# Storing the filter features by residue instead of in order of position

## The chip, the cores and the metric

The kernel runs on one core of a Trainium2 chip. The metric is the device time of one execution in microseconds; lower is better.

## The reference

One layer of a hybrid block on x (1 x 2048 x 1024): RMS norm, an input projection to 3072 columns, a short convolution, a second-order Hyena operator (two long convolutions by FFT with generated filters, each multiplied by a gate), a multi-scale pooling branch, and an output projection with a residual. The change touches the generation of the filters only:

```python
    h = jnp.sin(freq * (z @ w1 + b1))
    h = jnp.sin(freq * (h @ w2 + b2))
    h = jnp.sin(freq * (h @ w3 + b3))
    h = (h @ w_proj).reshape(L, HYENA_ORDER, N_DIRECTIONS, HYENA_WIDTH)
    ...
    return h * decay[:, None, None, :]
```

`h` before its last product are the features: 64 numbers for each of L = 2048 positions. Each position's features times `w_proj` (64 x 2048) and times a decay give the filters of two orders, two directions and 512 channels, which then go through the FFT.

## The kernel before

The work goes in this order: the projection with its pooling and gate parts (to about 400 us), the rest of the projection in natural layout with the short convolution (lines 493 to 571, to about 600 us), and then the long convolutions, in four units of an order and a half of the channels (lines 795 to 837), with the output projection of the pooling branch (`fill`, lines 783 to 793) spread between. A planner places the instructions in each engine's queue by priorities, data and its own estimates, so lines of different parts are interleaved; each engine runs its queue in order.

The features are computed early (`mlp`, line 433) and kept in DRAM as `h_d`. While the third block of the natural projection runs (`ch == 2`, lines 495 to 507), they are read back in four pieces of 512 positions, on both halves of the partitions: partitions 0 to 63 of the table `HT` get the features rounded to fp32r (ScalarE, line 506), partitions 64 to 127 the remainder of that rounding (VectorE, line 507). `HT` holds the positions in order, with 16 columns of zero behind them (line 497). The staging tile `hb` has one buffer, whose place a split weight half (line 230) uses before and after.

The FFT wants position 16 a + r by residue r. So `pre_k` (line 606) generates for residue n2 with a stationary operand of 128 columns at a step of 16, one for each direction, and the two halves of the split weights:

```python
                    c0 = n2 if dr == 0 else 16 - n2
                    lh = HT[:, c0:c0 + 2033:16]
                    for k_, wt in enumerate((wh, wl)):
                        T.matmul(ps[:, dr], lh, wt[:, dr * 256:dr * 256 + 256], start=(k_ == 0), stop=(k_ == 1))
```

These four matmuls (the group of one residue) fill one PSUM bank `gen` of 128x512. VectorE multiplies it by the decay into `ab` (line 631); two residues make a pass `m`, of which GpSimd forms the sum (line 635) and VectorE the difference (line 636) of the directions; two products with the transform matrix `f1` follow (`s1k`, line 643), one evacuated by ScalarE and one by VectorE (line 644). `gen` and `s1k` share two PSUM banks (tag "k"). After eight passes VectorE transposes the result in 32x32 blocks (line 604) and the unit's loop over frequencies (`gloop`, lines 669 to 718: `pk`, `px`, `pc`) begins. In the first unit the passes stand nearly alone; in the others they are interleaved with `gloop`, with the next stage's transforms (`s`, `py`) and with `fill` (`fp`).

The natural projection itself (`nm`, lines 540 to 542) is 24 matmuls of 128x256 for each of 16 row blocks, in a ring of six PSUM banks, evacuated by three products on VectorE (line 547). The convolution's neighbours over the block's edge come by two shifted row loads (`a0p`, line 550, `a2p`, line 556), issued by the queue of SyncE as soon as VectorE has made their source.

Of the kernel before, what the change touches and what calls it, by code (L numbers as in the profile page):

```python
# [10 lines left out]
F32 = mybir.dt.float32  # L11
F32R = mybir.dt.float32r
I32 = mybir.dt.int32
AF = mybir.ActivationFunctionType
ALU = mybir.AluOpType

P = 128
L = 2048
# [3 lines left out]
R = 16  # L22
# [126 lines left out]
def build(tc, I, out, debug=None):  # L149
    nc = tc.nc  # L150
    V, S, G, T, Q = nc.vector, nc.scalar, nc.gpsimd, nc.tensor, nc.sync
# [334 lines left out]


    hp = pool(hst, "hp", 1, None, "right")
    HT = hp.tile([P, L + 16], F32R, name="HT")
    nat = ExitStack()  # L490
    sn = pool(nat, "sn", 1, None, "right")
    psN = pool(nat, "psN", 1, PS, "right")
    for ch in range(4):
        load_w(ci)
        if ch == 2:

            V.memset(HT[:, L:L + 16].bitcast(F32), 0.0)
            for b in range(2):
                for q in range(2):
                    hb = sn.tile([P, 2, 512], F32R, tag="wh4", name=f"hb{b}{q}", bufs=1)  # L500
                    hs, hh = hb[:, 0].bitcast(F32), hb[:, 1]
                    for hf in range(2):
                        S.dma_start(out=hs[64 * hf:64 * hf + 64], in_=h_d[64 * b:64 * b + 64, q * 512:q * 512 + 512])
                    sl = slice(b * 1024 + q * 512, b * 1024 + q * 512 + 512)
                    S.copy(out=hh, in_=hs)
                    S.copy(out=HT[0:64, sl], in_=hh[0:64])
                    V.tensor_tensor(out=HT[64:128, sl], in0=hs[64:128], in1=hh[64:128], op=ALU.subtract)
        wc = sn.tile([P, 4, 256], F32, tag="wc", name=f"wc{ch}", bufs=1)
        for s in range(3):
            Q.dma_start(out=wc[:, s], in_=I["cw"][s:s + 1, ch * 256:ch * 256 + 256].broadcast_to([P, 256]))  # L510
        Q.dma_start(out=wc[:, 3], in_=I["cb"][:, ch * 256:ch * 256 + 256].broadcast_to([P, 256]))
        dst = g0_d[ch % 2]

        def store(r, t):

            if ch > 1:
                Q.dma_start(out=dst[:, r:r + 4], in_=t)
                return
            hi = sn.tile([P, 4, 256], F32R, tag="vh", name=f"vh{ch}_{r}", bufs=1)
            S.copy(out=hi, in_=t)  # L520
            G.tensor_tensor(out=t, in0=t, in1=hi, op=ALU.subtract)
            for k, a in enumerate((hi.bitcast(F32), t)):
                for i in range(2):
                    for c in range(2):
                        Q.dma_start(out=v_d[ch, r // 2 + i, c, :, k],
                                    in_=a[:, 2 * i:2 * i + 2, 128 * c:128 * c + 128])

        a0p = sn.tile([P, 256], F32, tag="a0p", name=f"a0p{ch}", bufs=1)
        a2p = sn.tile([P, 256], F32, tag="a2p", name=f"a2p{ch}", bufs=1)
        t15 = sn.tile([P, 256], F32, tag="t15", name=f"t15{ch}", bufs=1)  # L530
        G.memset(a0p, 0.0)
        G.memset(a2p, 0.0)
        prev0 = prevt = ot = pot = None
        for l2 in [15] + list(range(15)):
            ps = psN.tile([P, 256], F32, tag="nm", name=f"nm{ch}_{l2}", bufs=6)
            xh, xl = XH[l2 // 4], XL[l2 // 4]
            ls = slice((l2 % 4) * 128, (l2 % 4) * 128 + 128)
            for d in range(NT):
                wh, wl = wcache[ci][0][d]
                T.matmul(ps, xh[:, d, ls], wh, start=(d == 0), stop=False)  # L540
                T.matmul(ps, xh[:, d, ls], wl, start=False, stop=False)  # L541
                T.matmul(ps, xl[:, d, ls], wh, start=False, stop=(d == NT - 1))  # L542
            if l2 == 0:
                load_w(ci + 1, sn)
            a = [sn.tile([P, 256], F32, tag=f"a{s}", name=f"a{s}_{ch}_{l2}", bufs=(3, 1, 3)[s]) for s in range(3)]
            for s in range(3):
                V.scalar_tensor_tensor(out=a[s], in0=ps, scalar=r_nat[:, l2:l2 + 1], in1=wc[:, s],  # L547
                                       op0=ALU.mult, op1=ALU.mult)
            if l2 == 15:
                Q.dma_start(out=a0p[1:128], in_=a[0][0:127])  # L550
                G.tensor_tensor(out=t15, in0=a[1], in1=wc[:, 3], op=ALU.add)
                a2_15 = sn.tile([P, 256], F32, tag="a215", name=f"a215{ch}", bufs=1)
                S.copy(out=a2_15, in_=a[2])
                continue
            if l2 == 0:
                Q.dma_start(out=a2p[0:127], in_=a[2][1:128])
            if l2 % 4 == 0:
                ot = sn.tile([P, 4, 256], F32, tag="ot", name=f"ot{ch}_{l2}", bufs=2)
            tt = sn.tile([P, 256], F32, tag="tt", name=f"tt{ch}_{l2}", bufs=3)
            V.tensor_tensor(out=tt, in0=a[1], in1=wc[:, 3], op=ALU.add)  # L560
            G.tensor_tensor(out=tt, in0=tt, in1=(a0p if l2 == 0 else prev0), op=ALU.add)
            if l2 > 0:
                G.tensor_tensor(out=pot[:, (l2 - 1) % 4], in0=prevt, in1=a[2], op=ALU.add)
                if l2 % 4 == 0:
                    store(l2 - 4, pot)
            prev0, prevt, pot = a[0], tt, ot
        G.tensor_tensor(out=pot[:, 2], in0=prevt, in1=a2_15, op=ALU.add)
        G.tensor_tensor(out=t15, in0=t15, in1=prev0, op=ALU.add)
        G.tensor_tensor(out=pot[:, 3], in0=t15, in1=a2p, op=ALU.add)
        store(12, pot)  # L570
        ci += 1
# [29 lines left out]
    def trans(B, cbs=range(8)):  # L601
        for cb in cbs:
            ap = B[:, :, cb * 32:cb * 32 + 32].rearrange("p a c i -> p c a i")
            V.transpose(out=ap, in_=ap)  # L604

    def pre_k(o, hf):
        u = f"{o}{hf}"
        kw = wp.tile([P, 1024], F32, tag="wraw", name=f"kw{u}", bufs=1)
        wr, hd = kw[:, 0:512], kw[0:1, 512:768]
        for h in range(2):  # L610
            Q.dma_start(out=wr[64 * h:64 * h + 64].rearrange("p (a c) -> p a c", a=2), in_=I["fwo"][:, o, :, hf])
        Q.dma_start(out=hd, in_=I["hd"][o:o + 1, hf * 256:hf * 256 + 256])
        wh = hp.tile([P, 512], F32R, tag="kwh", name=f"kwh{u}", bufs=1)
        wl = hp.tile([P, 512], F32R, tag="kwl", name=f"kwl{u}", bufs=1)
        S.copy(out=wh, in_=wr)
        V.tensor_tensor(out=wl, in0=wr, in1=wh, op=ALU.subtract)
        sds = {}

        def gen(m):
            dc = kp.tile([P, 2, 2, 256], F32, tag="dec", name=f"dec{u}_{m}", bufs=2)  # L620
            (S if u == "00" and m < 2 else Q).dma_start(out=dc, in_=I["t_dec"][hf, m])
            ab = abp.tile([P, 2, 2, 256], F32, tag="ab", name=f"ab{u}_{m}", bufs=2)
            for i in range(2):
                n2 = 2 * m + i
                ps = psB.tile([P, 2, 256], F32, tag="k", name=f"gen{u}_{n2}", bufs=2)
                for dr in range(2):
                    c0 = n2 if dr == 0 else 16 - n2
                    lh = HT[:, c0:c0 + 2033:16]
                    for k_, wt in enumerate((wh, wl)):
                        T.matmul(ps[:, dr], lh, wt[:, dr * 256:dr * 256 + 256], start=(k_ == 0), stop=(k_ == 1))  # L630
                V.tensor_tensor(out=ab[:, i], in0=ps, in1=dc[:, i], op=ALU.mult)  # L631
                if n2 == 0:
                    G.tensor_tensor(out=ab[0:1, 0, 0], in0=ab[0:1, 0, 0], in1=hd, op=ALU.add)
            sd = wp.tile([P, 2, 2, 256], F32, tag="wh", name=f"sd{u}_{m}", bufs=3)
            G.tensor_tensor(out=sd[:, 0], in0=ab[:, :, 0], in1=ab[:, :, 1], op=ALU.add)  # L635
            V.tensor_tensor(out=sd[:, 1], in0=ab[:, :, 0], in1=ab[:, :, 1], op=ALU.subtract)
            sds[m] = sd

        def s1k(m):
            sd = sds.pop(m)  # L640
            for ri in range(2):
                ps = psB.tile([P, 2, 256], F32, tag="k", name=f"s1k{u}_{m}_{ri}", bufs=2)
                T.matmul(ps, f1[:, ri], sd[:, ri], start=True, stop=True)  # L643
                (V.tensor_copy if ri else S.copy)(out=BK[:, ri * 8 + m].rearrange("p c i -> p i c"), in_=ps)

        for m in range(9):
            if m < 8:
                gen(m)
            if m:
                s1k(m - 1)  # L650
        trans(BK)
# [171 lines left out]
    op = pool(ost, "op", 1, None, "right")  # L823
# [122 lines left out]
```

## Time and profile before

| | us |
|---|---|
| median of 3 runs | 1264.46 (1262.76 to 1265.32) |
| the profiled execution | 1265.64, of which its span 1263.9 |
| TensorE busy | 1179.0 (93%) |
| VectorE busy | 860.1 (68%) |
| ScalarE busy | 440.3 (35%) |
| GpSimd busy | 469.6 (37%) |
| mean granted TensorE clock | 0.980 |

The busy time of TensorE counts matmuls that overlap, so 93% does not mean that the array is at its peak. Weight loads are listed as an engine of their own (PEld) and run beside the matmul before them. What a stage is worth is read from the chain of work that ended last and from the timeline of that stage. In the rows, L630 is line 630; `gen<-kwl,HT` is an instruction that writes the tile `gen` from `kwl` and `HT`; "x4" merges four of a kind; what stands in brackets is how long the engine was idle before it and who ended that.

### The profile page before, as it was taken

The page shows a single profiled execution, that of the slowest core. Times are in us where ns is not written, and L with a number is a line of the kernel's source. Part 1 is how long each engine was busy: PE and PEld are TensorE (multiplying, and loading weights), DVE is VectorE, ACT ScalarE, POOL GpSimd, SP SyncE. Part 2 cuts the span into 40 slices and gives each one's busy share as a digit, 9 for nine tenths or more (in the row PEclk, how much of TensorE's full clock was granted, in tenths as well). Part 3 has the DMA queues.
Part 4 walks back from the last instruction along what each step waited for, and adds up shares of the span by engine and source line. Part 5 has one row for each costly group of instructions (what it writes and reads, how often), then busy time and mean ns, then how long its engine had stood idle before and what let it go on. Part 6 is the DMA issues. An engine that isn't in the chain of part 4 may idle for free.

```text
span 1263.9 us, 16966 instructions
## 1 busy us (share of the span) xinstructions
PE 1179.0 (93%) x6040; PEld 974.8 (77%) x6040; DVE 860.1 (68%) x1419; ACT 440.3 (35%) x724; POOL 469.6 (37%) x416
## 2 busy tenths in 40 slices
PE   8799999999999999899979999999999999988894
PEld 6688888787887999899666786778777767677683
DVE  6865347446346567576678887784868874769887
ACT  7612111112112111100148463742375624833321
POOL 3202021404452477566515332421234321434544
PEclk9899999999999999999999999999999999999997
DMA  7214131321341353423675346537664457554764
GB/s 256 86 37 132 34 100 40 118 87 59 128 153 51 117 140 91 142 95 140 238 234 156 97 136 192 136 95 251 194 176 107 123 185 233 116 181 145 244 215 147
DMA packets 110628, 177.25 MB, mean 140 GB/s; under 512 B 11076, under 2 KB 58960, under 8 KB 109264
## 3 DMA queue, kind: packets, MB, share of 16 engines
q1 hardware_dynamic: 108720, 173.20, 44.6%
q10 hardware_dynamic: 1648, 2.44, 0.6%
q8 instruction: 48, 0.79, 0.3%
q0 software_dynamic: 176, 0.53, 0.1%
q14 instruction: 36, 0.29, 0.1%
HBM read 113.75 MB, written 44.56 MB: 125 GB/s over the span
## 4 chain that ended last, share of the span: by engine, by line
PE 58%; DVE 16%; DMA 10%; issue 7%; ACT 4%; POOL 4%; SPq 1%; DVEq 0%; ACTq 0%; POOLq 0%
PE mm L317 8%; PE mm L319 8%; PE mm L318 8%; PE gen L630 4%; PE pc L704 3%; PE s1k L643 3%; DMA a2p<-a 3%; PE pk L678 3%; PE px L690 2%; PE fp L768 2%; PE nm L540 2%; PE nm L542 2%; PE nm L541 2%; PE fp L769 2%; PE fp L770 2%
## 5 line engine op out<-in xcount | busy, mean ns | idle before, releaser
L540 PE MATMUL nm<-wh,XH 128*128 128x256 f32 x512 | 145.9, 285 | 6.0 <-DVE a L547 5.2
L542 PE MATMUL nm<-wh,XL 128*128 128x256 f32 x512 | 145.5, 284 | 0.0
L541 PE MATMUL nm<-wl,XH 128*128 128x256 f32 x512 | 145.2, 284 | 0.0
L696 POOL TENSOR_TENSOR xs<-xs,kk 128x512 f32<-128x512 f32 x64 | 84.8, 1328 | 118.9 <-ACT xs L693 81.5
L547 DVE SCALAR_TENSOR_TENSOR a<-nm,r_nat,wc 128x256 f32<-128x256 f32 x192 | 81.5, 475 | 50.0 <-DMA wc<-cw 14.6
L540 PEld LDWEIGHTS nm<-wh,XH 128*128 128x128 f32 x512 | 97.9, 191 | 6.9 <-DVE a L547 6.0
L317 PE MATMUL mm<-XH,wh 128*128 128x512 f32 x256 | 103.0, 403 | 0.0
L319 PE MATMUL mm<-XH,wl 128*128 128x512 f32 x256 | 102.2, 399 | 0.0
L635 POOL TENSOR_TENSOR sd<-ab 128x512 f32<-128x512 f32 x32 | 53.0, 1656 | 131.4 <-DVE ab L631 131.0
L318 PE MATMUL mm<-XL,wh 128*128 128x512 f32 x256 | 101.5, 396 | 0.0
L541 PEld LDWEIGHTS nm<-wl,XH 128*128 128x128 f32 x512 | 97.9, 191 | 0.0
L542 PEld LDWEIGHTS nm<-wh,XL 128*128 128x128 f32 x512 | 97.7, 191 | 0.0
L704 PE MATMUL pc<-yt,gi 128*128 128x256 f32 x256 | 69.7, 395 | 13.3 <-DVE BS L705 8.3
L604 DVE STREAM_TRANSPOSE BS<-BS 128x1024 f32<-128x1024 f32 x64 | 73.5, 1210 | 8.5 <-ACT BS L659 8.5
L695 DVE TENSOR_TENSOR yt<-px,kk 128x512 f32<-128x512 f32 x64 | 44.0, 688 | 43.1 <-ACT xs L693 24.6
L690 PE MATMUL px<-BS,gf 128*128 128x256 f32 x256 | 70.2, 395 | 3.1 <-DVE yt L695 1.6
L678 PE MATMUL pk<-BK,gf 128*128 128x256 f32 x256 | 70.9, 389 | 0.0
L704 PEld LDWEIGHTS pc<-yt,gi 128*128 128x128 f32 x256 | 45.0, 191 | 32.7 <-DVE BS L705 15.7
L659 ACT COPY BS<-s 128x512 f32<-128x512 f32 x64 | 39.9, 629 | 83.1 <-PE s L588 79.4
L643 PE MATMUL s1k<-sd,f 128*128 128x512 f32 x128 | 63.2, 603 | 2.6 <-POOL sd L635 2.6
L697 DVE TENSOR_TENSOR yt<-yt,xs 128x512 f32<-128x512 f32 x64 | 53.9, 843 | 12.9 <-POOL xs L696 10.7
L317 PE MATMUL mm<-XH,whz 128*128 128x512 f32 x128 | 54.2, 424 | 9.0 <-ACT XH L284 5.3
(208 smaller groups left out, 3153.3 us busy)
## 6 DMA issues: line engine op xcount, KB each, us to landing
kk<-kk SPq DMA_DIRECT2D x128, 128.0 KB
fy<-yp_d SPq DMA_DIRECT2D x32, 512.0 KB
dec<-t_dec SPq DMA_DIRECT2D x30, 512.0 KB
wr<-w SPq DMA_DIRECT2D x16, 512.0 KB
ut<-v_d SPq DMA_DIRECT2D x32, 256.0 KB
gt<-g_d SPq DMA_DIRECT2D x32, 256.0 KB
op_d<-fo SPq DMA_DIRECT2D x32, 256.0 KB
o<-op_d SPq DMA_DIRECT2D x32, 256.0 KB
```

Of the source, the lines that this page charges most:

```text
L317: T.matmul(ps, wh, XH[lb][:, d], start=(d == 0), stop=False)
L318: T.matmul(ps, wh, XL[lb][:, d], start=False, stop=False)
L319: T.matmul(ps, wl, XH[lb][:, d], start=False, stop=(d == NT - 1))
L540: T.matmul(ps, xh[:, d, ls], wh, start=(d == 0), stop=False)
L541: T.matmul(ps, xh[:, d, ls], wl, start=False, stop=False)
L542: T.matmul(ps, xl[:, d, ls], wh, start=False, stop=(d == NT - 1))
L547: V.scalar_tensor_tensor(out=a[s], in0=ps, scalar=r_nat[:, l2:l2 + 1], in1=wc[:, s], op0=ALU.mult, op1=ALU.mult)
L643: T.matmul(ps, f1[:, ri], sd[:, ri], start=True, stop=True)
L678: T.matmul(pk[:, i], gf[:, gs[m] + i], BK[:, gs[m] // 2, :, i], start=True, stop=True)
L690: T.matmul(px[:, i], gf[:, gs[m] + i], BS[:, gs[m] // 2, :, i], start=True, stop=True)
L696: G.tensor_tensor(out=xs, in0=xs, in1=kk[:, 1], op=ALU.mult)
L704: ins = T.matmul(pc[:, i], gi[:, gs[m] + i], yt[:, i], start=True, stop=True)
```

## The change

The table `HT` becomes 16 rows of 129 columns: column a of row r is position 16 a + r. The 129th column of row 0 is set to zero; of the other rows it is neither written nor read. The copies that fill the table read their piece with a step of 16 positions and write 32 neighbouring columns of each of the 16 rows. The stationary operand of `gen` is then 128 neighbouring columns of one row, beginning at column 0, or at column 1 of row 0 for position 16. The values, the number of instructions and the size of the table (2064 columns) stay as they are.

```diff
--- before.py
+++ after.py
@@ -486,7 +486,7 @@
 
 
     hp = pool(hst, "hp", 1, None, "right")
-    HT = hp.tile([P, L + 16], F32R, name="HT")
+    HT = hp.tile([P, R, 129], F32R, name="HT")
     nat = ExitStack()
     sn = pool(nat, "sn", 1, None, "right")
     psN = pool(nat, "psN", 1, PS, "right")
@@ -494,17 +494,18 @@
         load_w(ci)
         if ch == 2:
 
-            V.memset(HT[:, L:L + 16].bitcast(F32), 0.0)
+            V.memset(HT[:, 0, 128:129].bitcast(F32), 0.0)
             for b in range(2):
                 for q in range(2):
                     hb = sn.tile([P, 2, 512], F32R, tag="wh4", name=f"hb{b}{q}", bufs=1)
                     hs, hh = hb[:, 0].bitcast(F32), hb[:, 1]
                     for hf in range(2):
                         S.dma_start(out=hs[64 * hf:64 * hf + 64], in_=h_d[64 * b:64 * b + 64, q * 512:q * 512 + 512])
-                    sl = slice(b * 1024 + q * 512, b * 1024 + q * 512 + 512)
+                    sl = slice(b * 64 + q * 32, b * 64 + q * 32 + 32)
                     S.copy(out=hh, in_=hs)
-                    S.copy(out=HT[0:64, sl], in_=hh[0:64])
-                    V.tensor_tensor(out=HT[64:128, sl], in0=hs[64:128], in1=hh[64:128], op=ALU.subtract)
+                    hs, hh = (a.rearrange("p (l r) -> p r l", r=R) for a in (hs, hh))
+                    S.copy(out=HT[0:64, :, sl], in_=hh[0:64])
+                    V.tensor_tensor(out=HT[64:128, :, sl], in0=hs[64:128], in1=hh[64:128], op=ALU.subtract)
         wc = sn.tile([P, 4, 256], F32, tag="wc", name=f"wc{ch}", bufs=1)
         for s in range(3):
             Q.dma_start(out=wc[:, s], in_=I["cw"][s:s + 1, ch * 256:ch * 256 + 256].broadcast_to([P, 256]))
@@ -625,7 +626,7 @@
                 ps = psB.tile([P, 2, 256], F32, tag="k", name=f"gen{u}_{n2}", bufs=2)
                 for dr in range(2):
                     c0 = n2 if dr == 0 else 16 - n2
-                    lh = HT[:, c0:c0 + 2033:16]
+                    lh = HT[:, c0 % R, c0 // R:c0 // R + 128]
                     for k_, wt in enumerate((wh, wl)):
                         T.matmul(ps[:, dr], lh, wt[:, dr * 256:dr * 256 + 256], start=(k_ == 0), stop=(k_ == 1))
                 V.tensor_tensor(out=ab[:, i], in0=ps, in1=dc[:, i], op=ALU.mult)
```

## Rows read from the trace of the kernel before

**Rows 1.** Page, chain that ended last: share of the span by engine.

```profile
PE 58%; DVE 16%; DMA 10%; issue 7%; ACT 4%; POOL 4%; SPq 1%; DVEq 0%; ACTq 0%; POOLq 0%
```

**Rows 2.** Weight loads by line and shape: count, busy us, mean ns, idle before.

```profile
L541 PEld LDWEIGHTS nm<-wl,XH 128*128 128x128 f32 x512 | 97.9, 191 | 0.0
...
L630 PEld LDWEIGHTS gen<-kwl,HT 128*128 128x128 f32 x128 | 39.9, 312 | 0.5
...
L755 PEld LDWEIGHTS py<-f,BS 128*128 128x128 f32 x128 | 21.8, 211 | 0.1
```

**Rows 3.** Windows: length, busy us (count) per engine, granted clock, DMA share, GB/s.

```profile
560.00:590.00 30.00, 30.00 (x257) 30.00 (x256) 18.09 (x44) 0.41 (x1) 17.41 (x24) 1.00 0.31 105
612.00:622.00 10.00, 10.00 (x32) 5.99 (x31) 6.92 (x10) 2.52 (x4) 4.60 (x3) 1.00 0.85 307
670.00:690.00 20.00, 16.91 (x73) 12.93 (x72) 18.27 (x24) 16.13 (x28) 9.68 (x8) 1.00 0.65 171
536.60:540.60 4.00, 4.00 (x22) 4.00 (x23) 3.71 (x8) 2.29 (x3) 3.38 (x4) 0.57 0.22 89
```

**Rows 4.** Chain in order of time: start us, us, what.

```profile
522.13 13.79 DMA a2p<-a
...
763.38 1.72 PE s1k L643 x4
...
767.60 1.72 PE s1k L643 x4
...
1000.60 1.78 PE gen L630 x8
```

**Rows 5.** Chain by line: 602-1045, 602-637, 740-800, 800-875, 875-920, 1000-1045 us, in order.

```profile
by line: PE gen L630 10.1%; PE s1k L643 8.8%; issue 8.5%; PE pc L704 6.9%; PE pk L678 5.8%; PE px L690 5.8%; PE fp L768 3.8%; PE fp L769 3.5%; PE fp L770 3.4%; DVE BS L604 3.1%; PE s L586 2.5%; POOL sd L635 2.4%; PE s L588 2.4%; POOL xs L69
...
by line: PE gen L630 44.0%; PE s1k L643 37.9%; POOL sd L635 4.9%; PE s L586 3.5%; PE s L587 3.1%; PE s L588 3.0%; DVE ab L631 2.0%; DVE a L547 1.1%; issue 1.0%; POOLq L635 0.0%
...
by line: PE gen L630 16.1%; PE s1k L643 15.2%; PE fp L768 9.2%; PE fp L769 8.1%; PE fp L770 7.8%; issue 7.2%; PE pk L678 6.6%; POOL xs L696 5.0%; PE s L586 4.1%; POOL sd L635 3.6%; PE s L587 3.2%; PE s L588 3.2%; PE px L690 3.0%; PE py L588
...
by line: PE pc L704 18.1%; PE pk L678 12.1%; PE px L690 12.1%; DVE BS L604 12.1%; PE py L754 5.4%; PE py L755 5.0%; DMA ut<-v_d 4.9%; DMA y_d<-gt 4.9%; DMA gt<-g_d 4.8%; issue 3.6%; PE gen L630 2.9%; DVE gt L756 2.5%; DVE yt L697 2.3%; PE s
...
by line: PE gen L630 17.5%; PE s1k L643 17.0%; PE fp L768 12.5%; PE fp L770 11.4%; PE fp L769 10.9%; DMA kk<-kk 10.0%; DMA ut<-v_d 8.2%; PE px L690 4.0%; POOL sd L635 3.5%; PE s L586 2.1%; PE pk L678 2.0%; PE s L588 1.6%; PE s L587 1.6%; DV
...
by line: PE gen L630 19.5%; PE s1k L643 17.9%; DMA fy<-yp_d 12.2%; PE fp L768 8.8%; PE fp L769 8.3%; PE fp L770 7.8%; POOL sd L635 3.8%; DVE dd L732 3.7%; ACT fo L792 3.1%; PE s L587 2.9%; PE s L586 2.9%; PE s L588 2.7%; ACT BS L659 2.4%; P
```

**Rows 6.** Timeline of the first filter generation: start us, us, instruction, idle before.

```profile
606.10 3.70 POOL L635 TENSOR_TENSOR sd<-ab 128x512 f32<-128x512 f32 x2
...
611.27 0.69 DVE L631 TENSOR_TENSOR ab<-gen,dec 128x512 f32<-128x512 f32 x1 [0.60 <-DMA dec<-t_dec]
...
617.92 0.49 PE L630 MATMUL gen<-kwh,HT 128*128 128x256 f32 x1
...
619.17 0.69 DVE L631 TENSOR_TENSOR ab<-gen,dec 128x512 f32<-128x512 f32 x1 [0.35 <-PE gen L630]
...
620.01 1.95 PE L643 MATMUL s1k<-sd,f 128*128 128x512 f32 x4
...
621.14 0.63 ACT L644 COPY BK<-s1k 128x512 f32<-128x512 f32 x1 [3.27 <-PE s1k L643]
...
621.82 0.49 PE L630 MATMUL gen<-kwh,HT 128*128 128x256 f32 x1
```

**Rows 7.** Line 507, all four: ns min/median/max, first and last start.

```profile
L507 DVE TENSOR_TENSOR HT<-hb x4: 690/1058/2474, 516.0 to 538.4; 64x512 fp32r<-64x512 f32 x4
```

**Rows 8.** Timeline around the table's building: GpSimd and VectorE.

```profile
515.54 2.39 POOL L521 TENSOR_TENSOR ot<-ot,vh 128x1024 f32<-128x1024 f32 x1 [1.16 <-ACT vh L520]
...
516.01 2.47 DVE L507 TENSOR_TENSOR HT<-hb 64x512 fp32r<-64x512 f32 x1 [5.61 <-ACT hb L505]
...
529.72 1.27 DVE L547 SCALAR_TENSOR_TENSOR a<-nm,r_nat,wc 128x256 f32<-128x256 f32 x3 [2.97 <-DMA a0p<-a]
...
535.95 0.48 DVE L547 SCALAR_TENSOR_TENSOR a<-nm,r_nat,wc 128x256 f32<-128x256 f32 x1 [1.49 <-DMA a2p<-a]
```

## The prediction, made before the change was run

> **What bounds the kernel now.** I read the chain of work first: TensorE carries 58% of it, VectorE 16%, DMA 10% [rows 1]. So shorter TensorE work can shorten the kernel, but only where TensorE is what ends last. Then I compared the weight loads of line 630, the filter generation, with others of the same shape: 312 ns against 191 ns for the loads of line 541, whose 128 columns lie side by side, and 211 ns for line 755, whose columns lie two elements apart [rows 2]. The columns of line 630 lie 16 elements (64 bytes) apart. What counts is not a load's length but how often a matmul starts. In the dense projection 257 matmuls of 128x256 with a fresh weight load each start in 30.00 us, one every 0.117 us, at a granted clock of 1.00, that is at the 2.4 GHz level [rows 3]. Eight matmuls of line 630 with the same moving width take 1.78 us on the chain, one every 0.2225 us [rows 4]. The matmul isn't wider, so the wider spacing comes from the load. Last I asked the chain where these matmuls stand on it. Between 602 and 1045 us they are 10.1% of 443 us, 44.7 us [rows 5]; all 256 of them take 256 x 0.2225 = 57 us of TensorE. About three quarters are on the chain, but a chain that follows a busy engine back doesn't say that what feeds that engine is much earlier, so each stretch has to be looked at.
>
> **The change part by part.** (a) With the columns side by side, the spacing of line 630 should fall from 0.2225 to the 0.117 us of the projection, by 0.105 us a matmul: 0.42 us for a group of four (one residue, one direction pair, one PSUM bank), and 256 x 0.105 = 26.9 us of TensorE for all. This is the upper bound of the gain; the lower is nothing, if all of it lies beside other waits.
>
> (b) First stretch, 602 to 637 us: 15.4 us of the chain by its share of 44.0% [rows 5], 47% of which (0.105/0.2225) would be 7.2 us. But here each pass is a ring through one PSUM bank: from the first matmul of a group at 617.92, the VectorE product at 619.17, the transform's matmuls at 620.01, ScalarE's copy at 621.14, and the next group in that bank at 621.82 [rows 6]. One ring is 3.90 us; it contains only one of the pass's two groups, so it falls by 0.42 to 3.48 us. TensorE's own work per pass becomes 8 x 0.117 plus the 1.95 us of line 643, 2.9 us, so the ring stays the bound. The first pass gains nothing: its sums on GpSimd start at 606.10 and take 3.70 us for two behind older work of that engine [rows 6]. Next comes a product that waited 0.60 us for its decay table [rows 6], so I give that pass 0.35 us. Four rings then give 4 x 0.42 = 1.7, and the last pass, in which both groups stand one behind the other before the last product, 0.84. Sum 2.9 us. Behind it stand loads on a DMA system that was busy 0.85 of 612 to 622 us at 307 GB/s [rows 3]; the same transfers in 3.48 instead of 3.90 us would ask for some 12% more, 0.95. I let 2.0 of the 2.9 us through (bounds 0 and 2.9).
>
> (c) Later stretches, by share of the chain: 740 to 800 us, 16.1% of 60 = 9.7 us; 800 to 875, 2.9% of 75 = 2.2; 875 to 920, 17.5% of 45 = 7.9; 1000 to 1045, 19.5% of 45 = 8.8 [rows 5]. Together 28.6 us; 47% of them is 13.4 us. With the first stretch that is 44.0 of the 44.7 us; the remaining 0.7 us gives 0.3. Not all of it survives. In the densest passes, as from 763.38 to 767.60, a pass is 4.22 us [rows 4]; less 0.84 it would be 3.38, under the 3.48 us of the ring, so 0.1 us is lost in each of some seven such passes, 0.7 us. And between the groups lie steps set by VectorE and by the single bank of the output projection, which I price at a fifth of the rest: an estimate, bounded by 0 and by everything outside the dense passes. (13.4 - 0.7) x 0.8 = 10.2 us.
>
> (d) Building the table. The two copies and the subtraction read with a 64-byte step, in four pieces. No row shows VectorE or ScalarE at that step; the nearest is the weight load, whose spacing grows by 0.2225/0.117 = 1.9. Lower bound 0, upper bound one more hold-up like the one seen: the first subtraction took 2.47 us at 516.01 because GpSimd's 2.39 us operation was in its way, while the shortest of the four took 0.69 [rows 7, 8]. I take 1.9 times, +0.6 us each. The first is on the chain: VectorE's products for the projection queue behind it, and from one of them goes the shifted row load, issued 522.13 and 13.79 us long [rows 4], which holds VectorE and through it TensorE. So +0.6 us there (0 to 2.5). The second and third are followed by 2.97 and 1.49 us in which VectorE waits for such loads [rows 8], which cover 0.6 us; without this cover each would cost its 0.6. The fourth has no such gap but TensorE then has up to six banks queued, so it costs nothing unless VectorE falls behind. ScalarE's four copies of the same size would also double, beside a ScalarE that has little else there; if it had, the split of the next weights would wait for them. The memset of the edge is one column instead of 16; the table keeps 2064 elements, and no DMA, queue or wait is added or moved. The ring of loads into the staging buffer gets up to 0.6 us longer per piece, 2.4 us over all; the split of a weight half that uses the same buffer next comes that much later, and only the next block of 256 channels needs it.
>
> A page of the Trainium skill bears on (d) and speaks against the change: "SBUF — State Buffer", section "Door 1: The DMA port swizzle", has SBUF read in 16-byte lines, with a penalty for each access to a new line. The weight loads agree (191, 211 and 312 ns at steps of 4, 8 and 64 bytes); no row here shows it for the copies, which by that page would now pay what the matmuls paid 256 times over; the sum is as above, since its factor is that of the loads.
>
> **The rivals.** First, TensorE alone is the bound: (b) and (c) give in full what the chain's shares say, 7.2 + 13.4 + 0.3 - 0.6 = 20.3 us, so 1264.5 - 20.3 = 1244. For it: from 612 to 622 us TensorE was busy for all 10.00 us [rows 3]. Against it: the ring of [rows 6]. Second, cover: only the seven dense passes keep their 0.74 us each, 5.2, and half of 2.0 comes through from the first stretch: 5.2 + 1.0 - 0.6 = 5.6 us, 1259. For it: VectorE's transposes and the loads between the stages sit at fixed places. Third, the change doesn't do what it says: the load's length is not from the step but, say, from the tile or from a start that moves with the residue, and only (d) is left: 1265. Against it, the 211 ns at a step of two [rows 2]. The Trainium skill, "TensorE: Matmul & The Clock Gate", section "LDWEIGHTS", would end there too: it lets the time of a load depend on the number of its columns alone, 107 ns for 128 at any step. The 312 beside 191 ns at the same 128 columns disagrees.
>
> Fourth, slower: the shorter groups leave TensorE waiting for the banks, and its clock falls to the lower of its two levels (1.2 GHz). The place is the passes of (b) and (c); the price is read where TensorE had just waited for those row loads: in 536.6 to 540.6 us the granted clock was 0.57 [rows 3], 0.43 x 4.0 = 1.7 us lost per fall. It decides from eight falls on; ten would give 17 us against 12 gained, 1269. Against it: from 670 to 690 us TensorE was busy 16.91 of 20 us at a granted 1.00 [rows 3], 85%, and the new ring leaves it at 2.9/3.48 = 83%.
>
> **How the numbers follow.** Forecast: 2.0 + 10.2 + 0.3 - 0.6 = 11.9 us off the profiled execution of 1265.64 us (its span is 1263.9), so 1253.7; it lies 1.2 us above the median of the runs, and against that median of 1264.46 the time is 1252.5 us. Chances: forecast 0.54, TensorE alone 0.16, cover 0.20, no effect 0.06, slower 0.04. The range runs from 1242, below the first rival, to 1260.5, above the second; left out are the third and fourth and about 0.08 at the ends. A change under 0.2%, 2.5 us, can't be told from none here: faster by more 0.88, within it 0.08, slower by more 0.04 (the last 0.02 of cover's lower tail falls to no change).
>
> **What would show it.** Weight loads of line 630 near 191 ns and eight of its matmuls in some 0.94 us show (a); a pass in the first stretch of about 3.5 us shows (b), 3.1 would favour the first rival. The subtraction of line 507 at 1.3 us where nothing holds it shows (d). Granted clock under 1.00 in 602 to 637 or 740 to 776 us would show the fourth. The forecast is wrong if the stages behind the passes (transposes, the output projection's loads) end at their old times, or if the planner, which places the generation's work among other work by its own estimates, orders these stretches otherwise.

## The result, and the profile after

The changed kernel took 1249.43 us (median of 4 runs, 1248.65 to 1252.21), the kernel before beside it 1263.61 us (4 runs, 1258.06 to 1265.32). The ratio is 0.9898, 95% interval 0.9873 to 0.9924: 12.9 us less (9.6 to 16.0). Two more sets of runs of the same pair gave 0.9905 (0.9886 to 0.9924) and 0.9885 (0.9855 to 0.9915). The forecast was 11.9 us less. The profiled execution of the changed kernel took 1252.21 us, with a span of 1250.4 us. Every engine's queue holds the same instructions in the same order as before; only the shapes of the table's three kinds of writes and of the weight load differ. Lines from 506 on have moved down by one.

First the weight load and the spacing. Weight loads by line and shape (the view of [rows 2]: busy us, mean ns, then idle before them and its releaser):

```profile
L631 PEld LDWEIGHTS gen<-kwl,HT 128*128 128x128 f32 x128 | 24.1, 188 | 1.2 <-issue 0.5
L631 PEld LDWEIGHTS gen<-kwh,HT 128*128 128x128 f32 x128 | 24.0, 188 | 17.1 <-ACT BK L645 10.3 <-DVE BK L645 3.8 <-issue 2.2
```

The load went from 312 to 188 ns, what the projection's loads take. Timeline of the first filter generation (start us, us, instruction, idle before), the lines that answer [rows 6]:

```profile
618.75 0.39 PE L631 MATMUL gen<-kwh,HT 128*128 128x256 f32 x1
...
618.97 0.28 PE L631 MATMUL gen<-kwl,HT 128*128 128x256 f32 x1
...
619.09 0.28 PE L631 MATMUL gen<-kwh,HT 128*128 128x256 f32 x1
...
619.21 0.28 PE L631 MATMUL gen<-kwl,HT 128*128 128x256 f32 x1
619.58 0.69 DVE L632 TENSOR_TENSOR ab<-gen,dec 128x512 f32<-128x512 f32 x1
...
620.42 1.95 PE L644 MATMUL s1k<-sd,f 128*128 128x512 f32 x4
...
621.55 0.63 ACT L645 COPY BK<-s1k 128x512 f32<-128x512 f32 x1 [2.86 <-PE s1k L644]
622.24 0.19 PEld L631 LDWEIGHTS gen<-kwh,HT 128*128 128x128 f32 x1 [0.69 <-ACT BK L645]
622.24 0.39 PE L631 MATMUL gen<-kwh,HT 128*128 128x256 f32 x1
```

The second matmul of a group starts 0.22 us after the first, and the others 0.12 us apart. From the group at 618.75 to the next in its bank at 622.24 is 3.49 us, against 3.90 in [rows 6]; the three steps behind the group (product, transform, copy) take as long as before. What the other bank does is new on the chain of work (start us, us, what):

```profile
616.94 1.97 PE s1k L644 x4
618.93 0.70 DVE BK L645
619.67 0.74 PE gen L631 x4
620.42 1.97 PE s1k L644 x4
```

The second group waits for VectorE's copy out of the bank the transform has just used. TensorE now idles in each pass: busy 9.27 us of 612 to 622 where it had been 10.00 [rows 3], while the DMA share rose from 0.85 to 0.94:

```profile
612.00:622.00 10.00, 9.27 (x38) 5.00 (x36) 7.63 (x12) 2.33 (x4) 4.22 (x3) 1.00 0.94 343
```

The page's chain by engine, the line that answers [rows 1]:

```profile
PE 54%; DVE 18%; DMA 10%; issue 8%; ACT 5%; POOL 5%; SPq 1%; DVEq 0%; POOLq 0%; ACTq 0%
```

The chain by line for 602-1045, 740-800, 800-875, 875-920 and 1000-1045 us, in this order, answering [rows 5]:

```profile
by line: issue 9.2%; PE s1k L644 8.1%; PE pc L705 6.9%; PE pk L679 6.2%; PE px L691 5.7%; PE fp L769 4.1%; PE gen L631 3.9%; DMA fy<-yp_d 3.6%; DMA dec<-t_dec 3.6%; PE fp L770 3.4%; PE fp L771 3.3%; POOL sd L636 2.4%; PE s L587 2.4%; PE s L
...
by line: PE s1k L644 13.8%; DMA fy<-yp_d 9.3%; PE pk L679 9.1%; PE gen L631 7.9%; PE fp L769 7.7%; issue 7.1%; PE fp L770 6.6%; PE fp L771 6.2%; POOL xs L697 5.0%; PE px L691 4.4%; POOL sd L636 3.6%; PE s L587 3.6%; PE s L589 3.4%; PE s L58
...
by line: PE pc L705 16.4%; PE pk L679 12.0%; PE px L691 10.9%; PE py L755 8.3%; PE py L756 7.5%; DMA y_d<-gt 4.8%; DMA ut<-v_d 4.5%; PE s1k L644 4.0%; DMA gt<-g_d 3.8%; PE s L587 3.2%; PE gen L631 3.2%; PE s L589 2.7%; PE s L588 2.5%; DVE y
...
by line: PE s1k L644 17.6%; PE fp L769 13.5%; DMA kk<-kk 10.3%; PE fp L771 9.8%; PE fp L770 9.7%; PE gen L631 7.4%; issue 6.8%; DVE yt L698 5.5%; PE px L691 4.0%; POOL sd L636 3.5%; POOL xs L697 2.9%; PE pc L705 2.5%; PE pk L679 2.0%; DVE a
...
by line: DMA dec<-t_dec 13.0%; DMA fy<-yp_d 11.6%; PE s1k L644 10.7%; DVE BS L605 10.1%; PE fp L769 7.4%; PE fp L770 6.4%; PE fp L771 6.0%; DVE ab L632 6.0%; POOL sd L636 3.8%; DVE dd L733 3.7%; PE gen L631 3.5%; PE s L589 2.5%; PE s L588 2
```

Generation fell from 10.1% to 3.9% of 602 to 1045 us. Where it left the chain, loads took part of its place in this trace: the output projection's `fy` from 740 to 800 us (9.3% of 60 = 5.6 us), the decay table from 1000 to 1045 (13.0% of 45 = 5.9 us).

The densest passes of the later stretches, 4.22 us in [rows 4], are now 3.48 us (chain in order of time: start us, us, what):

```profile
760.14 1.72 PE s1k L644 x4
...
763.62 1.72 PE s1k L644 x4
```

Last the building of the table. Line 508 and ScalarE's copy of line 507 by source (ns min/median/max, first and last start), answering [rows 7]:

```profile
L507 ACT CAST HT<-hb x4: 1091/1099/1106, 517.2 to 539.0; 64x512 fp32r<-64x512 f32 x4
L508 DVE TENSOR_TENSOR HT<-hb x4: 1082/1294/2849, 517.2 to 540.0; 64x512 fp32r<-64x512 f32 x4
```

VectorE's timeline around it, answering [rows 8]:

```profile
517.21 2.85 DVE L508 TENSOR_TENSOR HT<-hb 64x512 fp32r<-64x512 f32 x1 [5.61 <-ACT hb L505]
...
526.27 1.08 DVE L508 TENSOR_TENSOR HT<-hb 64x512 fp32r<-64x512 f32 x1 [2.46 <-ACT hb L505]
...
531.24 1.27 DVE L548 SCALAR_TENSOR_TENSOR a<-nm,r_nat,wc 128x256 f32<-128x256 f32 x3 [3.04 <-DMA a0p<-a]
...
537.63 0.48 DVE L548 SCALAR_TENSOR_TENSOR a<-nm,r_nat,wc 128x256 f32<-128x256 f32 x1 [1.96 <-DMA a2p<-a]
```

The free subtraction went from 0.69 to 1.08 us (1.57 times), the one held up by GpSimd from 2.47 to 2.85 us. Before, ScalarE's copy took 0.62 us in each of four pieces; it now takes 1.10 (1.76 times). The waits behind the second and third piece, 2.97 and 1.49 us in [rows 8], are still there at 3.04 and 1.96 us. The shifted row load `a2p`, issued 6.12 us after the first subtraction's start in [rows 4, 8] (516.01 and 522.13), now comes 6.55 us after it (517.21 and 523.76):

```profile
523.76 13.84 DMA a2p<-a
```

### The profile page after: what moved, and what is told of

Read it like the earlier page. It is cut to its first block, busy times and chain, and to the rows that moved or that the text cites. A ratio compares the mean times of both kernels' runs of the same rounds, so it can differ in the third digit from the quotient of the medians.

```text
span 1250.4 us, 16966 instructions
## 1 busy us (share of the span) xinstructions
PE 1156.9 (93%) x6040; PEld 945.9 (76%) x6040; DVE 859.8 (69%) x1419; ACT 440.6 (35%) x724; POOL 469.5 (38%) x416
## 4 chain that ended last, share of the span: by engine, by line
PE 54%; DVE 18%; DMA 10%; issue 8%; ACT 5%; POOL 5%; SPq 1%; DVEq 0%; POOLq 0%; ACTq 0%
PE mm L317 7%; PE mm L319 7%; PE mm L318 7%; PE pc L705 3%; PE pk L679 3%; PE s1k L644 3%; PE nm L541 3%; PE nm L542 3%; PE nm L543 3%; PE px L691 3%; DMA a2p<-a 2%; PE fp L769 2%; PE fp L770 2%; PE fp L771 2%; DVE o L899 2%
## 5 line engine op out<-in xcount | busy, mean ns | idle before, releaser
L698 DVE TENSOR_TENSOR yt<-yt,xs 128x512 f32<-128x512 f32 x64 | 54.0, 844 | 14.0 <-POOL xs L697 11.9
```

## The experiments

The runs stand in three sets, each beside the kernel before on the same chip: the first four, the next four and the last three rows of the table. Differences are ratio minus one, times the median before (1262.11, 1262.21 and 1262.80 us in the three sets), with the 95% interval in brackets.

| run | edit | ratio | us against before |
|---|---|---|---|
| after_again | none | 0.9905 | -12.0 (-9.6 to -14.4) |
| read_only | flat table, all generations read side by side | 0.9896 | -13.1 (-10.7 to -15.7) |
| first_unit | flat table, first unit alone side by side | 0.9978 | -2.8 (-5.7 to +0.3) |
| other_units | flat table, three later units alone | 0.9916 | -10.6 (-6.7 to -14.5) |
| build_only | table by residue, read with step 16 | 1.0014 | +1.8 (-0.6 to +4.2) |
| step2 | read with a step of 2 | 0.9911 | -11.2 (-7.6 to -14.9) |
| step4 | read with a step of 4 | 1.0000 | 0.0 (-2.1 to +2.3) |
| ring | changed kernel, other banks in first unit | 0.9934 | -8.3 (-5.0 to -11.5) |
| after_third | none | 0.9885 | -14.5 (-10.7 to -18.3) |
| ring_dec | ring, one decay load issued elsewhere | 0.9900 | -12.6 (-8.6 to -16.5) |
| ring_dec_s | ring_dec, s transforms first | 0.9879 | -15.3 (-12.2 to -18.4) |

Two runs of the unaltered changed kernel stand as references beside the others of the first and the third set; the second set has none.

> The changed kernel unaltered, as the mark for the others of this series. All theories: about 1.0% below the kernel before (ratio 0.989 to 0.992), weight load of the generation 188 ns, its matmul pairs about 0.117 us apart, ring of the first unit 3.48 us.

> The changed kernel unaltered, beside the two that go on from the ring: 1249 to 1251 us, 0.8 to 1.1% below before.

after_third's median was 1247.33 us, under the 1249 that was expected; its ratio agrees with the other two sets.

**Is it the read, and which units bring what?** Three kernels keep the flat table and its cheap build, and let all, the first, or the three later units read 128 neighbouring columns. `first_unit` and `other_units` put the new line under a condition on the unit.

```diff
-                    lh = HT[:, c0:c0 + 2033:16]
+                    lh = HT[:, c0 * 120:c0 * 120 + 128]
```

> The table is built flat as before, and the generation reads 128 neighbouring columns of it from column 120*c0, so its features are the wrong ones; the order of the work is the changed kernel's. Theory T (the step of the load alone sets the pace, and the strided build costs 0.4 to 0.6 us): load 188 ns, ring 3.48 us, time 0.4 to 0.6 us below the changed kernel, so 13 us below before. Rival B (part of the gain, or of its size, comes from the new place of the table's writes): the gain is smaller than the changed kernel's by 2 us or more. Rival C (the strided build costs up to its bound of 2.5 us): 2 us or more below the changed kernel.

> The flat table as before; only the first unit's 16 generations (the stretch from 602 to 637 us) read neighbouring columns, and those of wrong positions; the other three units read with step 16. Theory T (a ring of two PSUM banks paces this stretch, which lets 2 to 3 us through): 2 to 4 us below before, weight load 188 ns in the first unit and 312 ns in the others. Rival R1 (TensorE alone sets the end, every saving counts in full): 64 matmuls x 0.105 = 6.7 us below before. Rival R2 (the loads of the decay table and the engines beside TensorE cover it): within 1 us of before.

> The counterpart: the first unit reads with step 16, the three other units read neighbouring columns of wrong positions. Theory T (chain share of the generation x 0.8 in the three later stretches): 9 to 11 us below before, and this gain and that of the first unit alone add up to the gain of the contiguous reading in all, within 1.5 us. Rival R1: 192 matmuls x 0.105 = 20 us below before. Rival R2 (given back at the spectra's loads at 740 to 800 us and at the output's stretch): 3 to 5 us below before. If the 2.9 us that the two traces show after 1035 us, where no generation stands, come from the clock or the loads and not from the edit, they are missing here and the gain is 7 us.

Weight loads by source: the two kinds of `read_only`, then one of `first_unit` (ns min/median/max).

```profile
L630 PEld LDWEIGHTS gen<-kwh,HT x128: 186/188/193, 600.0 to 1021.3; 128*128 128x128 f32 x128
L630 PEld LDWEIGHTS gen<-kwl,HT x128: 187/188/193, 600.1 to 1021.5; 128*128 128x128 f32 x128
```

```profile
L630 PEld LDWEIGHTS gen<-kwh,HT x128: 186/300/319, 598.9 to 1026.6; 128*128 128x128 f32 x128
```

`read_only` is within 1.1 us of the changed kernel in the same set, with the whole gain: the new place of the table's writes brings nothing that shows, which goes against rival B. Rival C, a build of 2 us or more, isn't excluded by these two intervals. The parts are -2.8 and -10.6, sum -13.4, against -13.1 for all: in the middle they add, as the theory said, though the intervals, some 3 and 4 us to each side, are wider than the 1.5 us that was asked for. TensorE alone (-6.7 and -20) is ended by `other_units`; -2.8 beside it is well short of -6.7 too. Full cover of the later units is ended by -10.6, whose interval lies outside its 3 to 5. Full cover of the first unit, within 1 us of before, the times don't exclude.

**The build by itself.** The table is the changed kernel's; generation reads it as one row with step 16. Since this read takes in the 129th column of every row, all 16 of them are set to zero.

```diff
-                    lh = HT[:, c0 % R, c0 // R:c0 // R + 128]
+                    lh = HT.rearrange("p r a -> p (r a)")[:, c0:c0 + 2033:16]
```

> The table is built by residue as in the change, with strided writes, and the generation reads it as one flat row with step 16, so its features are the wrong ones. Theory T: the ScalarE copies into the table 1.10 us for 0.62, the VectorE subtractions 1.1 for 0.7 us, load 312 ns, and the time 0.2 to 1 us above before. Rival C (the strided build delays what follows on VectorE in full): 1.5 to 2.5 us above before. Rival B (the new place of the table's writes brings a part of the gain): 1 us or more below before.

Source rows of `build_only`:

```profile
L507 ACT CAST HT<-hb x4: 1067/1094/1122, 517.2 to 539.2; 64x512 fp32r<-64x512 f32 x4
L508 DVE TENSOR_TENSOR HT<-hb x4: 1082/1516/2820, 517.2 to 539.9; 64x512 fp32r<-64x512 f32 x4
...
L631 PEld LDWEIGHTS gen<-kwh,HT x128: 291/314/331, 603.2 to 1034.6; 128*128 128x128 f32 x128
```

+1.8 us (-0.6 to +4.2): not the gain of 1 us or more that rival B wants, so it falls here; whether the build costs 0.6 or 2.5 us the times don't tell. The traces narrow it. From the start of the first subtraction to the issue of `a2p`, which waits for the products behind it, the seven traces with the 64-byte copies take 6.5 to 6.6 us, the six with a flat table or runs of 8 or 16 bytes 6.0 to 6.3; the means, 6.55 and 6.15 us, differ by 0.4. That is the price on the path that the forecast named, where it put 0.6. Over a longer stretch the difference is of the same size but less clear. I took the start of the same ScalarE instructions in each trace, one before the build (505.2 us in the kernel before) and one after it (567.6 us), and looked at how the distance changed against the kernel before. In the seven traces it grew by 0.2, 0.9, 0.9, 0.1, 1.0, 1.0 and 0.9 us, mean 0.7; in the five others by 0.3, 0.6, 0.2, -0.1 and -0.1, mean 0.2. The difference is some 0.5 us; two traces of the seven, those of the changed kernel's first run and of `build_only`, show none of it.

**How far may the load stride?** The table by pairs or by groups of four residues, so that the load's columns lie 2 or 4 elements apart.

```diff
-    HT = hp.tile([P, R, 129], F32R, name="HT")
+    HT = hp.tile([P, R // 4, 129, 4], F32R, name="HT")
...
-                    lh = HT[:, c0 % R, c0 // R:c0 // R + 128]
+                    lh = HT[:, c0 % R // 4, c0 // R:c0 // R + 128, c0 % 4]
```

> The table by pairs of residues, so that the generation's weight load reads with a step of 2 elements (8 bytes). Theory T in the form of the Trainium skill's page on SBUF (16-byte lines of the read port; two hits or more in a line): load 188 to 215 ns and time as the changed kernel's within 2 us. Rival P (the load's time grows in proportion to the bytes it strides over): load well above 200 ns, near 196 at step 2 if the 124 ns between step 1 and 16 are spread evenly over the steps. Rival S (any step but 1 falls back to the slow load): load 312 ns, time as before.

> The table by groups of four residues: the weight load reads with a step of 4 elements (16 bytes). By 16-byte lines with one element in each: load 312 ns, pairs 0.2225 us apart, time as before plus or minus 2 us. Rival F (a step of up to 4 elements is free): load 188 ns, time as the changed kernel's. Rival P (even growth with the step): load 213 ns, about 80% of the gain kept.

`step2`, then `step4`, by source:

```profile
L631 PEld LDWEIGHTS gen<-kwh,HT x128: 192/196/330, 599.5 to 1019.0; 128*128 128x128 f32 x128
...
L507 ACT CAST HT<-hb x4: 628/643/647, 513.3 to 534.4; 64x512 fp32r<-64x512 f32 x4
L508 DVE TENSOR_TENSOR HT<-hb x4: 689/1116/2467, 513.3 to 535.5; 64x512 fp32r<-64x512 f32 x4
```

```profile
L631 PEld LDWEIGHTS gen<-kwh,HT x128: 307/329/336, 603.4 to 1036.0; 128*128 128x128 f32 x128
...
L507 ACT CAST HT<-hb x4: 620/620/622, 516.5 to 538.0; 64x512 fp32r<-64x512 f32 x4
L508 DVE TENSOR_TENSOR HT<-hb x4: 689/898/2481, 516.5 to 539.2; 64x512 fp32r<-64x512 f32 x4
```

The load takes 188 ns at a step of 4 bytes, 196 at 8, 329 at 16 and 314 at 64 (medians). It is a cliff between 8 and 16 bytes (12 wasn't run), no growth with the step: at 8 bytes even growth wanted 196 ns as well, but at 16 it wanted 213. The time follows: the whole gain at a step of 2 elements, none at 4, with the same layout otherwise. The copies into the table show the same edge from the other side: reading four neighbours of every 64 bytes, or two, they cost what the flat ones do (0.62 and 0.64 us on ScalarE, 0.69 us for the shortest on VectorE); one element of every 64 costs 1.10 and 1.08 us.

The Trainium skill, "SBUF — State Buffer", section "Door 1: The DMA port swizzle", has 16-byte lines that want two hits or more each; 196 and 329 ns agree with that. It goes on that for fp32 a stride of 4 is free; the 329 ns disagree, if that is meant as a step of four elements. The Trainium skill, "TensorE: Matmul & The Clock Gate", section "LDWEIGHTS", lets the load depend on its columns alone; these four times at 128 columns disagree.

**Is the first stretch bound by the two banks?** Generation of the first unit moves to the two banks of tag `pk`, idle there, so that it and the transform don't take turns.

```diff
-                ps = psB.tile([P, 2, 256], F32, tag="k", name=f"gen{u}_{n2}", bufs=2)
+                ps = psB.tile([P, 2, 256], F32, tag="pk" if u == "00" else "k", name=f"gen{u}_{n2}", bufs=2)
```

> The changed kernel, with the first unit's generations in the two PSUM banks of the other tag, so that they and the stage-one transforms no longer take turns in two banks. Theory T (the two shared banks pace the first stretch at 3.48 us per pass): pass about 3.0 us, 2 to 4 us below the changed kernel. Rival D (the decay table's loads at 0.85 DMA share pace it): pass 3.4 us or more, time within 1 us of the changed kernel. Rival E (VectorE, which is queued with multiplication, subtraction and a copy in each pass, paces it): within 1 us, with VectorE over 85% busy in the stretch.

The banks did bound the passes, if not alone, and freeing them brought nothing in the end time: 8.3 us below before, less than the changed kernel in any of its three sets. Two marks, counted from the first generation's start in each trace, tell where it went: the last of ScalarE's copies of the unit, and the first matmul of the spectral product `px`, which needs both the generation and the s transforms.

| read of the load | last BK copy | first px |
|---|---|---|
| slow: before, step4, build_only, other_units | +33.6, +34.0, +34.2, +33.6 | +57.0, +56.7, +58.8, +56.1 |
| fast: after, after_again, after_third | +30.9, +30.9, +31.2 | +53.5, +54.0, +55.4 |
| fast: step2, read_only, first_unit | +30.5, +30.6, +30.8 | +52.9, +54.0, +53.0 |
| ring, ring_dec, ring_dec_s | +28.8, +28.4, +35.7 | +56.7, +55.6, +53.5 |

The change took 3.1 us out up to the last copy (means 33.9 and 30.8) and 3.4 up to `px`. `ring` took 2 us more out up to the copy (3.16 us a pass in the mean). The first two passes fall to 2.7 us; the next three take 3.7, 3.6 and 3.4, and there a decay load of 5.58 us, from 613.73, stands on the chain, so rival D is the next bound. Rival E falls, as VectorE was busy 14.78 of the 20 us from 610 to 630. In `ring`, `px` is 2.9 us later than the fast kernels' mean, so some 5 us were given back between. Its source rows for the two marks:

```profile
L645 ACT COPY BK<-s1k x8: 617/626/632, 607.7 to 629.8; 128x512 f32<-128x512 f32 x8
...
L691 PE MATMUL px<-BS,gf x64: 385/388/766, 657.7 to 702.6; 128*128 128x256 f32 x64
```

Windows of the stretch between them (busy us per engine; the last three columns are granted clock, DMA share, GB/s):

```profile
632.00:638.00 6.00, 4.09 (x24) 3.57 (x22) 6.00 (x6) 2.26 (x4) 0.00 (x0) 0.82 0.86 267
638.00:644.00 6.00, 5.13 (x24) 4.84 (x24) 6.00 (x7) 2.58 (x5) 0.00 (x0) 0.61 0.83 240
```

Its chain of work there (start us, us, what):

```profile
631.01 2.70 DMA ut<-v_d
...
634.82 4.04 DMA ut<-v_d
...
639.00 0.55 PE s L587
639.55 0.22 PE s L588
639.77 0.21 PE s L589
```

With the banks as a reason gone, the planner put the transforms of the signal (`s`) behind the generations: 24 of their matmuls stand ahead of the unit's last generation in the changed kernel, 7 here. They then wait for their loads, 2.70 and 4.04 us, and run at the lower clock: a granted 0.61 from 638 to 644 us, matmuls 0.21 us apart for 0.12 at full clock. So the edit changed the order of the work with the banks (at 856 of the 6040 places of TensorE's queue the trace has a matmul of other tiles than the changed kernel's), and as a test of the end time it is confounded. As a test of the pass it is less so: between the second and the fifth copy neither trace has an `s` matmul, and three passes take 3.48 or 3.49 us in the changed kernel and 2.7, 3.7 and 3.6 in `ring`. Two more runs undo the order in steps: `ring_dec` issues the unit's third decay load from ScalarE's queue too (150 places differ, counted in the same way), `ring_dec_s` also writes half of the `s` transforms ahead of the generation.

```diff
-            (S if u == "00" and m < 2 else Q).dma_start(out=dc, in_=I["t_dec"][hf, m])
+            (S if u == "00" and m < 3 else Q).dma_start(out=dc, in_=I["t_dec"][hf, m])
...
+    pre_s(0, 0, (0,))
     pre_k(*units[0])
...
-    pre_s(0, 0)
+    pre_s(0, 0, (1,))
```

> The first unit's generations in the other tag's PSUM banks, and the third decay load of that unit issued from ScalarE's queue, where the first two are. The order of the work stands nearer to the changed kernel's than in the ring run alone (26 places differ on TensorE against 92), but the s transforms of the first columns still come behind the generations. If the ring run was slow because of the order in the later stretches, this one is 2 to 4 us below the changed kernel; if the s transforms that come late, or the loads behind them, are what takes the gain back (DMA share over 0.8 from 612 to 660 us), it is within 2 us of the changed kernel or above it, with the same idle TensorE at 630 to 645 us.

> As the last, with the s transforms of the first half of the columns written ahead of the first unit's generations, so that they are not late. If the late s transforms took the ring's gain back: 2 to 5 us below the changed kernel, and no stretch at a lower clock at 632 to 644 us. If the loads (decay table, ut, gf and gi: about 12 MB by 660 us) set the end of the first stretch in any order: within 2 us of the changed kernel. If order alone decides, with nothing to say beforehand, as much as 5 us above it.

The same window of `ring_dec`, then of `ring_dec_s`:

```profile
632.00:638.00 6.00, 4.55 (x22) 4.11 (x21) 6.00 (x6) 1.90 (x3) 0.00 (x0) 0.62 0.78 232
```

```profile
632.00:638.00 6.00, 4.84 (x18) 2.51 (x17) 3.46 (x6) 1.86 (x3) 2.15 (x2) 1.00 0.89 272
```

The longest piece of the chain of `ring_dec_s` between 628 and 662 us:

```profile
642.70 6.88 DMA wo<-wo
```

`ring_dec` is 1.9 us above the changed kernel of its set. `ring_dec_s` is 0.8 us below it by the ratios and 0.7 above by the medians, which is no difference. Both intervals are some 3 to 4 us wide to each side, so "within 2 us" is their middle and not more. `ring_dec` keeps the clock's fall, and in `ring_dec_s` it comes later, beginning in the wait for `wo` (same columns as above):

```profile
646.00:655.00 9.00, 6.91 (x17) 5.10 (x18) 8.53 (x9) 4.70 (x8) 0.00 (x0) 0.62 0.79 259
```

By the marks neither brings `px` earlier than the changed kernel's +53.5 to +55.4. Whichever comes first, generation or `s` transforms, something else is late: `ut` in the one order, the weights `wo` in the other. Two things go with it, and no run takes them apart. The DMA share over the whole 600 to 660 us is 0.79 in both (0.70 before, 0.76 after). The granted clock over the same 60 us is 0.91 in `ring`, 0.89 in `ring_dec` and 0.91 in `ring_dec_s`, against 1.00, 1.00 and 0.97 in the changed kernel's three traces; by the sum that the fourth rival uses that is an estimate of 5 to 7 us lost, as far as it stood on the path. That the loads set the end of this stretch in any order fits all three; it is argued, not shown, since no run took loads away. Against the share of DMA as the whole reason stand `step2` and `first_unit`: 0.81 over these 60 us, and `px` at +52.9 and +53.0, the earliest of all. No kernel here beats the changed one by more than the runs can tell.

## Why the prediction was right, point by point

**(a) The spacing.** Forecast 0.117 us and near 191 ns; the trace has 0.12 us and 188 ns. `step4` shows that it is the step and nothing else of the new layout, which ends the third rival.

**(b) The first stretch.** The ring was forecast at 3.48 us and took 3.49, the first pass was to gain nothing and gained nothing (first copy of line 645 6.7 us after the first generation in both traces), and the sum of 2.9 us up to the last copy was 2.7 in this pair of traces and 3.1 in the mean of ten. The chain in the changed kernel goes round the other bank of the two (transform, VectorE's copy, second group), not round the one that was forecast. The forecast ring is as tight: the first group's product ends at 620.27 and the transform starts 0.15 us later, as it did before (619.86 and 620.01 in [rows 6]). Each of the two rings holds one group, so 0.42 us is what either loses. What was mis-sized is what passes on: 2.0 of 2.9 was let through, for fear of the loads, while up to `px` 3.4 us arrived in the traces and the time of `first_unit` fell by 2.8 us (between 5.7 less and 0.3 more, so 2.0 isn't excluded). The price of the loads did not show behind the changed kernel's passes; `ring`, which freed the banks, met late loads and a lower clock.

**(c) The later stretches.** Forecast 10.2 us; `other_units` took 10.6 off (6.7 to 14.5). That the middle comes so close is in part luck, since the first half of the step was off, and the second as far as the wide interval tells. The chain's share fell by more than the 13.4 us that the spacing alone explains: in the four stretches generation was 28.6 us, and is now 7.9% of 60, 3.2% of 75, 7.4% of 45 and 3.5% of 45, together 12.0 us, 16.6 less. Other traces agree: 11.4 to 13.8 us in the six traces with the fast read in the later units and the order of before, 28.0 to 28.6 in the three with the slow read in all units. More was given back than the fifth: of some 15 to 17 us 10.6 arrived, which leaves a third, but the interval of `other_units` allows anything from nothing to over half. Which load took generation's place differs from trace to trace. From 1000 to 1045 us the decay table's load stands on the chain in the changed kernel's first trace, and in neither `after_again` nor `after_third`, where generation keeps 3.6 us. From 740 to 800 us `fy` stands there with 5.6, 5.5 and 5.3 us in the three, but with 6.0 in `step4` as well, and not at all in `other_units`. So that something else becomes later than TensorE is shown; that it is these loads is not. (The windows are fixed, and the changed kernel is up to 10 us further on in the last one, so the shares carry that error.)

**(d) The build.** Factors 1.76 and 1.57 where 1.9 was taken, from a row of another engine. The price on the path, 0.6 us forecast, is 0.4 by the issue of `a2p`: the mechanism held and the factor was too large, as the first subtraction grew by 0.38 us. By the times the whole build lies between 0.6 less and 4.2 us more. The cover named for the second and third piece held: both waits are still there. The fourth piece, priced at nothing, stands on the chain with 1.5 us in five of the seven traces with the 64-byte copies and in none of the others, so its price isn't shown to be nothing.

**What was not foreseen** is in the pair of traces but not in the change. Matched ScalarE instructions show the changed kernel 1.4 us late at 567.6 us and 13.4 us early at the end, 3.6 of them gained after 1035 us, where no generation stands. Three kernels with the slow read through all later units (`first_unit`, `build_only`, `step4`) gain 2.5, 2.1 and 2.0 us there as well, and every trace with the fast read gains, if only 0.6 in `other_units`: it is the kernel before whose one profiled execution was slow in that stretch. Of the difference behind 567.6 us, 14.8 us, some 2 us are therefore the trace's own scatter. A difference of two profiled executions has such errors in each stretch; a stretch is worth believing when several kernels show it.

**The rivals.** TensorE alone (1244 us) and cover (1259) fall by `other_units`, no effect (1265) by `step4` and `step2` together. Slower by the clock (1269) did not happen: from 602 to 637 and from 760 to 776 us the changed kernel was granted 1.00. Behind the passes it has falls where the kernel before was granted 1.00, to 0.86 in 790 to 800 us (TensorE busy 7.85 us of 10) and 0.89 in 1030 to 1045, about 1.4 and 1.7 us by the sum of that rival. But the kernel before has two as well, at other places, of 1.7 us each by the same sum, and there the changed kernel was granted 1.00 (windows of the kernel before; the last three columns are granted clock, DMA share, GB/s):

```profile
660.00:664.00 4.00, 4.00 (x15) 3.43 (x13) 2.35 (x4) 2.44 (x5) 3.77 (x4) 0.57 1.02 363
1049.00:1053.00 4.00, 4.00 (x12) 3.17 (x11) 0.00 (x0) 0.00 (x0) 0.00 (x0) 0.57 0.48 184
```

And `first_unit`, whose later generations still read with the wide step, falls to 0.83 in 790 to 800 us too. So the falls aren't shown to come from the shorter groups, they are two and not eight, and in this pair of traces both kernels have as many. That a change of order can bring such falls `ring` shows, with 0.61 behind two waits for loads.

## What to carry to other kernels

Compare weight loads of one shape across a kernel's lines: here the one that took 1.6 times the others was read with a step, and its matmuls started 1.9 times as far apart. Lay the table out once, where it is written, so that elements that follow each other in the load lie at most 8 bytes apart; if the writer is the tighter place, runs of two elements make both sides cheap (196 ns and 0.64 us here). Then price the gain stretch by stretch from the ring that each pass runs in, and look for the load that comes next in line: here about a third of what generation gave up on the chain of the later stretches did not arrive in the time, by the middle of a wide interval.

## What the hardware showed that was not expected

- A step of 16 bytes is no better for a weight load than one of 64: 329 and 314 ns. Nearly all of the penalty is between 8 and 16 bytes.
- ScalarE and VectorE pay it as well, but less: 1.76 and 1.57 times for reading one 4-byte element of every 64 bytes, nothing for two or four neighbours of 64.
- A weight load whose rows start at a multiple of 516 bytes (the changed table) and one whose start moves by 480 bytes (`read_only`) both take 188 ns.
- The granted clock fell to 0.61 while TensorE still counted 5.13 us busy of 6 (638 to 644 us in `ring`), behind 6.7 us of waiting for two loads; busy time alone doesn't show such a stretch.
